# A two-layer decoder block on one core: the last sublayer's p product taken out of the expert loop and parked in DRAM, gates by f32r, one-hots turned by spread ranks

## The chip, the cores and the metric

The kernel runs on one core of one Trainium2 chip. The time is that of one execution on the device in microseconds (us); the time of the kernel before is the median of three runs. The profile is of one further execution, taken by the hardware profiler. In it PE is the matrix engine, PEld its weight loads, DVE the vector engine, ACT the scalar engine, POOL the general-purpose engine, and SP the engine that here does nothing but issue DMAs. A "q" behind a name (SPq) is that engine's sequencer.

## What is computed

Two transformer blocks of width 1024 over 512 tokens. The change lies in the second half of the second block: a mixture of experts (32 experts of hidden size 512 in 4 groups; each token goes to 2 experts of one group) and behind it a sublayer that adds a gated product of a second input `p` (256 features per token).

```python
x = x + merged @ w_out[i]                         # end of the mixer
h = rmsnorm_2(x, g_ffn[i])
x = x + hier_moe(h, w_grp[i], w_exp[i], w1[i], w3[i], w2[i])
h = rmsnorm_2(x, g_ple[i])
x = x + jax.nn.sigmoid(h @ w_pg[i]) * (p[i] @ w_ple[i])   # last sublayer
return rmsnorm_2(x, g_final)
```

`hier_moe` is, for each token, gate-weighted `(silu(x @ w1[e]) * (x @ w3[e])) @ w2[e]` over its two experts. The product `p @ w_ple` depends on inputs alone, so it may be computed at any time before the last sublayer.

## The kernel before

Activations lie feature-major: 8 tiles of 128 features x 512 tokens (`KT` is 8). Outside the experts a product is made of three matmuls of 4-byte operands in the reduced format f32r (`mm3`: high x high, low x high, high x low), after each operand has been split into a high and a low part: the high part by a cast on ACT, the low by a subtraction (`split`, `split_to`), on DVE unless told otherwise. `fm` makes one 128 x 512 output tile this way; with 8 input tiles it takes 24 matmuls, with 2 it takes 6. The raw weights come by SP into a ring of three tiles (`raw`), their halves lie in rings `wh` and `wl` of three.

Four stages bear on the change, in order of time:

- **End of the mixer.** For each of 8 output tiles `m`, `fm` multiplies by `w_out2`; `done(m)` adds the result to `X`, forms the normed tile `hf`, multiplies it by the router's weights (`logits`), turns it (`htr`, four transposes) and splits the turned tile into `ht` (ACT high, DVE low). Here a scheduler sets the order on every engine.
- **Router.** `ltr` turns the logits to token-major; a chain of some 35 small DVE operations picks group and experts (`first_max`), ends in the 0/1 matrix `Mb`, and after the `rank` matmuls gives `rk`, the place of each token in its expert's list, or a number over 900 where it is not in it. `GM` holds each token's gate for each expert and its norm.
- **Expert loop.** From here to the end of the loop PE's order is the order written in the code (`_InOrder`). Experts go in 16 pairs. `gather` compares `rk` with 0..63 for four experts, which gives the one-hots `dh` (tokens x slots), and multiplies `ht` by them (64 matmuls for a group of two pairs): the tokens of each expert in 64 slots, `xg`. Pair `p` then runs `hidden(p)` (`h`: with `w1` and `w3` as moving operand in full f32, two matmul instructions for each; two experts side by side in the columns of the array), `outputs(p-1)` (`y`, with `w2`), `hidden_turned(p)` (`hidt`), half of the next group's `gather`, half of the `combine` of the last two pairs (`comb`, which scatters the results back with `dt`, the turned one-hots, and adds them to `X`), `turned(p)` (`dtr`: four transposes of the one-hots and a DVE copy to `dt`), and `gates_of(p+1)` (`gate`: four f32 matmuls of the one-hots with the 33 columns of `GM`). In pairs 14 and 15, where no gather is left, its place is taken by `ple_proj`, the product `p @ w_ple` (`fm` of 24 matmuls in each), whose raw operands SP has loaded into the `raw` ring during the loop and DVE and ACT have split into three expert tiles.
- **Last sublayer.** `last` multiplies by `w_pg`, takes the sigmoid, multiplies by `ple[m]`, norms, and writes out.

The experts' weights are 192 blocks of 1 MB (12 for a pair), in the order of use. `expert_tile` deals out 11 tiles of 1 MB in turn (8 `slot`, 3 `aux`), so a block is loaded when the block 11 before it has been used. Blocks 0 to 16 are loaded ahead: 0, 1 and 4 to 12 into the 11 tiles, block 2 into an `x8` tile, 3 and 13 to 16 in halves into ring tiles that are free by then. All these loads stand in SP's one queue, in which an issue that waits for its tile holds up all behind it.

Of the kernel before, what the change touches and what calls it, by code (L numbers as in the profile page):

```python
# [20 lines left out]
P = 128  # L21
S = 512
# [24 lines left out]
CSTS = ["ident", "iota", "riota", "negones", "dist", "cdist", "rowok", "qscale"]  # L47
CSTN = [128, 64, 8, 128, 512, 4 * NCMP, 1, 4]
NKEPT = sum(CSTN[:3])
# [4 lines left out]
def _constants():  # L54
# [15 lines left out]
    put("iota", np.tile(np.arange(64), (P, 1)))  # L70
    put("riota", np.tile(8.0 - np.arange(8), (P, 1)))
# [105 lines left out]
def _build(ctx, tc, nc, A, out, probe, stop):  # L177
# [479 lines left out]
    def compress(i):  # L657
# [25 lines left out]
        gt = work.tile([P, 62], F32, tag="gelt", bufs=1, name="gelt")  # L683
# [603 lines left out]

    def done(m, pt):
# [13 lines left out]
        V.tensor_tensor(ht[1][:, :, fs], p3, ht[0][:, :, fs].bitcast(F32), ALU.subtract)  # L1302
# [11 lines left out]
    for m in range(KT):  # L1314
        done(m, fm(loadw(A["w_out2"][m]), y))
# [8 lines left out]

    rT = rt("rT")
# [5 lines left out]
    lfm = tmp("lfm")  # L1331
    SC.copy(lfm[:36], pl[:36])
    pt = s_ps("ltr")
    for t in range(4):
        T.transpose(pt[:, t * 36:t * 36 + 36], lfm[:36, t * P:t * P + P], ident[:36, :36])
    L = tmp("L")[:, :144].rearrange("p (t e) -> p t e", t=4)
    V.tensor_copy(L, pt[:, :144].rearrange("p (t e) -> p t e", t=4))

# [14 lines left out]
    gsel = rt("gsel", 4, 8)  # L1353
    V.tensor_tensor(gsel, L[:, :, 4:36].rearrange("p t (g e) -> p t g e", g=4),
                    goh.unsqueeze(3).to_broadcast([P, 4, 4, 8]), ALU.mult)
    sel = rt("sel", 8)
# [4 lines left out]
    oh12 = rt("oh12", 8)  # L1361
# [8 lines left out]
    pr = s_ps("rank")  # L1370
# [8 lines left out]


    pg = rt("pg")
    gd = rt("gd", 4)
# [15 lines left out]
    GM = rt("GM", NE + 1)  # L1398
    outer(GM[:, :, 0:NE], oh1)
    V.tensor_copy(GM[:, :, NE], rT)  # L1400
# [10 lines left out]
    slot_tags = itertools.cycle(4 * ["slot"] + na * ["aux"] + (ns - 4) * ["slot"])  # L1411

    def expert_tile(kt=4, c=512, dt=F32):
        return slot("mw", dt, next(slot_tags)).rearrange("p a b -> p (a b)").rearrange("p (k c) -> p k c", k=kt)
# [10 lines left out]
    def expert_load(ap):  # L1425
        w = expert_tile(*ap.shape[1:])
        nc.sync.dma_start(w, ap)
        return [w[:, k] for k in range(ap.shape[1])]
# [6 lines left out]

    def ring_tile(tag):
        return ring.tile([P, 1024], F32, tag=tag, bufs=3, name="mw")
# [9 lines left out]
    for n in (0, 1, 4, 5):  # L1447
        ahead[n] = expert_load(aps[n])
    ahead[3] += half_load(ring_tile("raw"), aps[3][:, 2:4])
    for n in range(6, 13):  # L1450
        ahead[n] = expert_load(aps[n])
# [314 lines left out]
```

## Time and profile before

| | us |
|---|---|
| median of three runs (1817.0 to 1819.53) | 1817.97 |
| profiled execution, own time | 1818.39 |
| its span (first to last instruction) | 1816.6 |
| PE busy | 1747.1 |
| PE loading weights (beside PE) | 1255.6 |
| DVE busy | 839.6 |
| ACT busy | 625.6 |
| POOL busy | 127.6 |

PE is busy 96% of the span, so the few stretches in which it waits, and the work that it does, are what time can come from. A matmul's own duration in the trace includes its way through the array, during which the next one already runs; the pace of a row of matmuls is read from the distance of their starts. The expert loop lies between about 1257 and 1746 us; DMA moves 12 to 13 MB for each pair of experts in it.

### The profile page before, as it was taken

What the parts mean: (1) busy time and instruction counts of PE and PEld (TensorE: products, weight loads), DVE (VectorE), ACT (ScalarE), POOL (GpSimd) and SP (SyncE); (2) the same over time, 40 slices, a digit from 0 to 9 for tenths busy, and PEclk for the clock granted to TensorE, in tenths of its full rate; (3) what the DMA queues carried; (4) which work ended last, traced back from release to release, by engine and by line L of the source; (5) the groups of instructions that cost most, each with busy time, mean ns of one, the idle gap of its engine ahead of it and who ended that gap; (6) DMA issues with size and microseconds to landing.
All of it is one profiled execution on the core that took longest, in us unless ns stands there. A gap on an engine that the chain in (4) does not pass through costs nothing. (4 is left out here: it accounts for less than half of the span.)

```text
span 1816.6 us, 22448 instructions
## 1 busy us (share of the span) xinstructions
PE 1747.1 (96%) x8936; PEld 1255.6 (69%) x8937; DVE 839.6 (46%) x1551; ACT 625.6 (34%) x1100; POOL 127.6 (7%) x152
## 2 busy tenths in 40 slices
PE   6999999899999999999999999997999999999896
PEld 4887777678888888888877887865454545454466
DVE  5676787895553333333653522743122222221256
ACT  4356777653332222222553434321110101011143
POOL 1100000551000000001100100200000000000030
PEclk9999999999999999999999999998999999999998
DMA  7532221773232333333531332345899999999831
GB/s 301 155 112 70 58 59 70 255 266 116 70 116 93 98 100 93 96 90 94 173 94 50 103 95 93 128 139 214 344 417 414 418 417 419 416 420 393 325 116 52
DMA packets 69998, 342.90 MB, mean 189 GB/s; under 512 B 7936, under 2 KB 10528, under 8 KB 45824
## 3 DMA queue, kind: packets, MB, share of 16 engines
q1 hardware_dynamic: 66736, 334.87, 50.0%
q0 software_dynamic: 2432, 5.77, 1.5%
q8 instruction: 72, 1.18, 0.3%
q10 hardware_dynamic: 720, 0.77, 0.1%
q14 instruction: 38, 0.31, 0.1%
HBM read 333.51 MB, written 2.10 MB: 185 GB/s over the span
## 5 line engine op out<-in xcount | busy, mean ns | idle before, releaser
L261 DVE TENSOR_TENSOR wl<-raw,wh 128x1024 fp32r<-128x1024 f32 (+1 forms) x185 | 238.5, 1291 | 297.8 <-ACT wh L261 294.0
L273 PE MATMUL fm<-hh,wh 128*128 128x512 f32 (+1 forms) x944 | 362.7, 385 | 3.6 <-ACT hh L467 2.0
L274 PE MATMUL fm<-hl,wh 128*128 128x512 f32 (+1 forms) x944 | 361.6, 383 | 2.1 <-DVE hl L468 1.6
L275 PE MATMUL fm<-hh,wl 128*128 128x512 f32 (+1 forms) x944 | 361.7, 384 | 1.1 <-DVE wl L261 1.1
L261 ACT CAST wh<-raw 128x1024 fp32r<-128x1024 f32 (+1 forms) x187 | 193.5, 1037 | 476.3 <-PE fm L274 264.9
L155 PE MATMUL h<-mw,x 128*64 128x512 f32 x1016 | 223.3, 594 | 0.0
L273 PEld LDWEIGHTS fm<-hh,wh 128*128 128x128 f32 x944 | 179.0, 190 | 39.1 <-issue 3.2
L275 PEld LDWEIGHTS fm<-hh,wl 128*128 128x128 f32 x944 | 178.7, 190 | 36.1 <-DVE wl L261 2.2
L274 PEld LDWEIGHTS fm<-hl,wh 128*128 128x128 f32 x944 | 179.0, 190 | 35.6 <-DVE hl L468 2.5
L155 PEld LDWEIGHTS h<-mw,x 128*64 128x64 f32 x1016 | 71.9, 137 | 135.6 <-issue 135.0
L155 PE MATMUL y<-mw,hT 128*64 128x512 f32 x512 | 115.2, 599 | 4.8 <-DMA mw<-in_w 4.8
L1540 DVE SCALAR_TENSOR_TENSOR hs<-h,gt,hs 128x512 f32<-128x512 f32 x16 | 12.0, 750 | 203.3 <-PE h L155 203.3
L155 PEld LDWEIGHTS y<-mw,hT 128*64 128x64 f32 x512 | 37.0, 139 | 79.4 <-issue 73.7
L1570 ACT CAST ywh<-y 128x512 fp32r<-128x512 f32 x30 | 17.6, 586 | 189.2 <-PE y L155 189.2
L1490 DVE TENSOR_TENSOR X<-comb,X 128x512 f32<-128x512 f32 x64 | 44.0, 690 | 62.8 <-PE comb L155 62.8
L1041 PE MATMUL fm<-hidh,wl 128*128 128x512 f32 (+1 forms) x188 | 71.8, 382 | 0.0
L1039 PE MATMUL fm<-hidh,wh 128*128 128x512 f32 (+1 forms) x188 | 71.6, 381 | 0.0
L1040 PE MATMUL fm<-hidl,wh 128*128 128x512 f32 (+1 forms) x188 | 71.6, 381 | 0.0
L234 ACT ACTIVATE hs<-h,gt 128x512 f32<-128x512 f32 x16 | 11.0, 687 | 173.0 <-PE h L155 173.0
L274 PE MATMUL tm<-wl,hh 128*128 128x512 f32 (+2 forms) x192 | 65.1, 339 | 2.5 <-DVE wl L261 2.5
L155 PE MATMUL gath<-dh,hh 128*128 128x256 f32 x256 | 64.4, 293 | 2.2 <-DVE cnt L1403 2.2
L275 PE MATMUL tm<-wh,hl 128*128 128x512 f32 (+2 forms) x192 | 65.3, 340 | 0.0
(434 smaller groups left out, 2786.4 us busy)
## 6 DMA issues: line engine op xcount, KB each, us to landing
mw<-in_w SPq DMA_DIRECT2D x186, 1024.0 KB, 10.7
wa<-in_w_ada SPq DMA_DIRECT2D x24, 1024.0 KB, 6.8
raw<-in_w_merge SPq DMA_DIRECT2D x32, 512.0 KB, 3.6
raw<-in_w_in SPq DMA_DIRECT2D x28, 512.0 KB, 3.9
raw<-in_w_gate SPq DMA_DIRECT2D x22, 512.0 KB, 3.5
raw<-in_w_up SPq DMA_DIRECT2D x22, 512.0 KB, 3.5
raw<-in_w_v SPq DMA_DIRECT2D x16, 512.0 KB, 3.6
raw<-in_w_proj SPq DMA_DIRECT2D x16, 512.0 KB, 3.6
```

Of the source, the lines that this page charges most:

```text
L155: self._put(self.eng.matmul(*a, **k))
L234: i = SC.activation(*a, **k)
L261: last_split[:] = copy(h, src).ins, sub(l, src, h.bitcast(F32)).ins
L273: T.matmul(pt, ah, bh, start=first, stop=False)
L274: T.matmul(pt, ah, bl, start=False, stop=False)
L275: T.matmul(pt, al, bh, start=False, stop=last)
L1039: T.matmul(pt[:, cs], wh[:, k], hid[0][:, n, cs], start=(n == 0), stop=False, skip_group_check=True)
L1040: T.matmul(pt[:, cs], wh[:, k], hid[1][:, n, cs], start=False, stop=False, skip_group_check=True)
L1041: T.matmul(pt[:, cs], wl[:, k], hid[0][:, n, cs], start=False, stop=(n == FT - 1), skip_group_check=True)
L1490: V.tensor_tensor(X[:, m], po, X[:, m], ALU.add)
L1540: V.scalar_tensor_tensor(hs, pt, st["gt"][:, 0:1], hs, ALU.mult, ALU.mult)
L1570: SC.copy(yh[:, n], ys[n])
```

## The change

- `ple_proj` moves from pairs 14 and 15 of the loop to the end of the mixer. It is a generator now, and `step` puts pieces of three matmuls between the last product of the mixer and the first gather: 6 matmuls before the last tile's `logits`, 3 before `ltr`, 21 before `rank`, 18 before `gather`. Its operands are loaded behind `w_out2` and split into the ordinary rings, the low parts by POOL. ACT copies each of the 8 result tiles into one slot tile and two `raw` tiles, and POOL writes them to a DRAM tile `pled` by eight DMAs of 256 KB. At the last sublayer SP reads `pled` back by two DMAs of 1 MB.
- PE's written order begins before `w_out2`, with `fm(m)` ahead of `done(m-1)`. `ltr` stands ahead of `ssT`, and the low part of `ht` for the last tile is made behind the first one-hots `dh0`, which are compared in four pieces.
- `gates_of`: `GM` is split into high and low f32r halves side by side, 66 columns, and multiplied by the one-hots in f32r: four matmuls. ACT copies the high half, DVE adds the low.
- `turned`: instead of transposing one-hots, the ranks are turned once (`rkT`, 32 experts x 512 tokens, in pair 0). For a pair, POOL spreads two columns of the identity over 64 columns each (`of`); one f32r matmul with `rkT` puts each expert's ranks on 64 partitions, and DVE compares them with the partition's number (`icol`) to give `dt`.
- The tiles of the expert weights are dealt in another order (`aux` first), and after the first 11 a twelfth block, in two `raw` halves, joins the turn.

```diff
+    def ple_proj():
+        raws = [load(a) for a in (A["p"], A["w_ple"][0], A["w_ple"][1])]
+        pf, *ws = [split(r, sub=G.tensor_sub) for r in raws]
+        t_ = slot("ple")
+        outs = [t_[:, i] for i in range(4)]
+        for t_ in (ring_tile("raw"), ring_tile("raw")):
+            outs += [t_[:, i * S:i * S + S] for i in range(2)]
+        for m in range(KT):
+            pt = next(banks)("ple")
+            for k in range(2):
+                n = 2 * (m % 4) + k
+                mm3(pt, ws[m // 4][0][:, n], ws[m // 4][1][:, n], pf[0][:, k], pf[1][:, k], k == 0, k == 1)
+                yield
+            SC.copy(outs[m], pt)
+            G.dma_start(pled[:, m], outs[m])
...
-    for m in range(KT):
-        done(m, fm(loadw(A["w_out2"][m]), y))
+    T = _InOrder(tc, nc.tensor)
+    pts = [fm(loadw(A["w_out2"][0]), y)]
+    for m in range(1, KT):
+        pts.append(fm(loadw(A["w_out2"][m]), y))
+        done(m - 1, pts[m - 1])
+
+    pler = ple_proj()
+    step(pler, 2)
+    done(KT - 1, pts[KT - 1])
+    step(pler, 1)
...
+    step(pler, 7)
...
+    dh0 = onehot()
+    for t in range(4):
+        i = V.tensor_tensor(dh0[:, t], rk[:, t, 0:4].unsqueeze(2).to_broadcast([P, 4, SLOTS]),
+                            K("iota").unsqueeze(1).to_broadcast([P, 4, SLOTS]), ALU.is_equal)
+    tc.add_manual_dep(subs[-1].ins, i.ins.name, order)
+    for _ in pler:
+        pass
...
+    GM = rout.tile([P, 4, 2 * (NE + 1)], F32R, name="GM")
+    V.tensor_copy(GM[:, :, :NE + 1], gm_)
+    V.tensor_tensor(GM[:, :, NE + 1:], gm_, GM[:, :, :NE + 1].bitcast(F32), ALU.subtract)
...
-    slot_tags = itertools.cycle(4 * ["slot"] + na * ["aux"] + (ns - 4) * ["slot"])
+    slot_tags = itertools.chain(na * ["aux"] + ns * ["slot"],
+                                itertools.cycle(na * ["aux"] + ns * ["slot"] + ["raw"]))
...
     def gates_of(p):
...
-            T.matmul(pgt[:, 0:NE + 1], dq[:, t].rearrange("p e s -> p (e s)"), GM[:, t],
+            T.matmul(pgt[:, 0:2 * n], dq[:, t].rearrange("p e s -> p (e s)"), GM[:, t],
                      start=(t == 0), stop=(t == 3))
+        gs = mix.tile([P, n], F32, tag="gs", bufs=1, name="gs")
+        SC.copy(gs, pgt[:, 0:n])
+        V.tensor_tensor(gs, pgt[:, n:2 * n], gs, ALU.add)
...
     def turned(p):
...
         pt = s_ps("dtr")
-        for t in range(4):
-            T.transpose(pt[:, t * P:t * P + P], dq[:, t].rearrange("p e s -> p (e s)"), ident)
+        of = tmp_r("of")[:, :P]
+        G.tensor_copy(of.rearrange("p (e s) -> p e s", e=2),
+                      ident[:, 2 * p:2 * p + 2].unsqueeze(2).to_broadcast([P, 2, SLOTS]))
+        T.matmul(pt, of, rkT, start=True, stop=True)
         pairs[p]["dt"] = mix.tile([P, S], F32R, tag="x2", bufs=3, name="dt")
-        V.tensor_copy(pairs[p]["dt"], pt)
+        V.tensor_scalar(pairs[p]["dt"], pt, K("icol"), None, ALU.is_equal)
...
-            nxt = gather(p // 2 + 1, sts[p // 2 + 1]) if p < NP - 2 else ple_proj(raws) if p < NP else iter(())
-        if p == NP - 4:
-            raws = ple_loads()
+            nxt = gather(p // 2 + 1, sts[p // 2 + 1]) if p < NP - 2 else iter(())
...
+    for i, t_ in enumerate((x8(4, S), expert_tile(4, S))):
+        nc.sync.dma_start(t_, pled[:, 4 * i:4 * i + 4])
+        ple.extend(t_[:, n] for n in range(4))
```

Three places of the built program show the moves. First PE from the last tile's `logits` to the first `gather`; before:

```order
L1295 MATMUL logits<-hf,wr 36x512
L1298 MATMUL htr<-cst,hf 128x128 x4
L1328 MATMUL ssT<-ones,acc 128x1 x4
L1335 MATMUL ltr<-cst,lfm 128x36 x4
L1373 LDWEIGHTS triub
L1373 MATMUL rank<-Mb,triub 128x32
...
L155 MATMUL gath<-dh,hh 128x256
```

and in the changed program, where each `ple` row that is shown stands for the first of its run (6, 3, 21 and 18 rows):

```order
L156 MATMUL ple<-wh 128x512
...
L156 MATMUL logits<-hf,wr 36x512
L159 MATMUL htr<-cst,hf 128x128 x4
L156 MATMUL ple<-wh 128x512
...
L159 MATMUL ltr<-cst,lfm 128x36 x4
L156 MATMUL ssT<-ones,acc 128x1 x4
L156 MATMUL ple<-wh 128x512
...
L156 MATMUL rank<-Mb,triub 128x32
...
L156 MATMUL ple<-wh 128x512
...
L156 MATMUL gath<-dh,hh 128x256
```

PE has matmuls of the p product between the steps for which it waited on DVE's chain before.

Second, PE at the end of the loop, from `hidt` of pair 14 to `h` of pair 15; before:

```order
L158 MATMUL hidt<-cst,hs 128x128 x4
L155 MATMUL fm<-mw 128x512 x24
L155 MATMUL comb<-dt,ywh 128x512
...
L158 MATMUL dtr<-cst,dh 128x128 x4
L155 MATMUL gate<-GM,dh 128x33 x4
```

and in the changed program:

```order
L159 MATMUL hidt<-cst,hs 128x128 x4
L156 MATMUL comb<-dt,ywh 128x512
...
L156 MATMUL dtr<-rkT,of 128x512
L156 MATMUL gate<-GM,dh 128x66 x4
```

The 24 matmuls of the p product are gone (as in pair 15), and the four transposes have become one matmul.

Third, SP's queue around the start of the loop, with what an issue waits for (DMAHW and DMASW are landings of transfers of the hardware queues and of POOL's software queue); before, with block 9 as `mw_9972` and the two halves of block 16 last among the loads ahead:

```order
L253 DMA raw_9812<-in_w_out2 128x1024 [waits DMAHW3_49,DVE_49]
L1433 DMA mw_9964<-in_w1 128x1024 [waits DMAHW5_49,DMAHW1_49,DVE_49]
...
L1427 DMA mw_9972<-in_w1 128x2048 [waits PE_49]
...
L1427 DMA mw_9978<-in_w3 128x2048 [waits DMAHW3_49,PE_49]
L1433 DMA mw_9992<-in_w2 128x1024 [waits DMAHW4_49]
L1433 DMA mw_9994<-in_w2 128x1024 [waits DMAHW5_49]
L1677 TENSOR_LOAD cnti_9949 [waits DVE_49,PE_49,Activation_49]
L1427 DMA mw_10218<-in_w2 128x2048 [waits DMAHW6_49,PE_49]
```

and in the changed program, with block 12 as `mw_10077` and the halves of block 13 as `mw_10079` and `mw_10081`:

```order
L254 DMA raw_9850<-in_w_ple 128x1024 [waits DMAHW3_49,DVE_49]
L1496 DMA mw_10061<-in_w3 128x2048 [waits Pool_49]
...
L1502 DMA mw_10067<-in_w1 128x1024 [waits DMAHW6_49,Pool_49]
L1496 DMA mw_10069<-in_w1 128x2048 [waits DMAHW4_49,PE_49]
...
L1496 DMA mw_10077<-in_w3 128x2048 [waits DMASW2_49,DMASW3_49,DMASW1_49,DMAHW0_49,DMASW0_49,Activation_49]
L1502 DMA mw_10079<-in_w3 128x1024 [waits DMASW5_49,DMAHW1_49,DMASW4_49,Activation_49]
L1502 DMA mw_10081<-in_w3 128x1024 [waits DMASW7_49,DMAHW2_49,DMASW6_49,Activation_49]
L1502 DMA mw_10083<-in_w3 128x1024 [waits DMAHW3_49,PE_49]
...
L1496 DMA mw_10328<-in_w2 128x2048 [waits DMAHW1_49,PE_49]
```

The loads of `p` and `w_ple` stand ahead of blocks 5 to 12, and blocks 12 to 16 stand behind the landing of the eight writes to `pled`. In the loop itself `p` and `w_ple` are no longer in the queue.

## Rows read from the trace of the kernel before

**Rows 1.** The page, part 1: busy time of each engine, share of the span, instructions.

```profile
PE 1747.1 (96%) x8936; PEld 1255.6 (69%) x8937; DVE 839.6 (46%) x1551; ACT 625.6 (34%) x1100; POOL 127.6 (7%) x152
```

**Rows 2.** Stretches: length; busy us by engine (PE, PEld, DVE, ACT, POOL); granted clock, DMA, GB/s.

```profile
1240.00:1250.00 10.00, 4.55 (x33) 4.48 (x34) 5.72 (x30) 1.70 (x3) 0.00 (x0) 0.50 0.48 195
1261.00:1311.00 50.00, 49.07 (x274) 23.43 (x272) 8.76 (x16) 4.89 (x8) 0.00 (x0) 1.00 0.85 329
1334.00:1666.00 332.00, 332.00 (x1763) 167.25 (x1762) 77.06 (x138) 33.34 (x55) 0.00 (x0) 1.00 1.01 417
1350.00:1360.00 10.00, 10.00 (x64) 6.30 (x61) 1.98 (x3) 2.33 (x4) 0.00 (x0) 1.00 1.02 425
```

**Rows 3.** PE's waits from 1180 us on: total, times, longest.

```profile
PE rank L1373 <- DVE Mb L1365: 5.6, 1, 5.6
PE y L155 <- DMA mw<-in_w: 4.8, 1, 4.8
PE gath L155 <- DVE cnt L1403: 2.2, 1, 2.2
PE logits L1295 <- DVE hf L1294: 1.3, 1, 1.3
```

**Rows 4.** PE in order of time, first gather: start, duration, instruction, count [idle before].

```profile
1246.00 0.55 PE L155 MATMUL gath<-dh,hh 128*128 128x256 f32 x1 [2.15 <-DVE cnt L1403]
...
1252.11 0.33 PE L155 MATMUL gath<-dh,hh 128*128 128x256 f32 x1
...
1256.36 0.97 PE L155 MATMUL gate<-GM,dh 128*128 128x33 f32 x8
```

**Rows 5.** PE in order of time, one pair in the middle of the loop.

```profile
1515.29 13.95 PE L155 MATMUL h<-mw,x 128*64 128x512 f32 x64
...
1536.45 0.36 PE L155 MATMUL gath<-dh,hh 128*128 128x256 f32 x1
...
1540.27 0.39 PE L155 MATMUL comb<-dt,ywh 128*128 128x512 f32 x1
...
1544.12 0.60 PE L158 MATMUL dtr<-cst,dh 128*128 128x128 f32 x4
1544.56 0.98 PE L155 MATMUL gate<-GM,dh 128*128 128x33 f32 x8
1545.47 13.95 PE L155 MATMUL h<-mw,x 128*64 128x512 f32 x64
```

**Rows 6.** PE in order of time, pairs 14 and 15.

```profile
1679.95 7.04 PE L155 MATMUL y<-mw,hT 128*64 128x512 f32 x32
...
1687.33 5.74 PE L155 MATMUL fm<-mw 128*128 128x512 f32 x24
1692.91 0.40 PE L155 MATMUL comb<-dt,ywh 128*128 128x512 f32 x1
...
1716.83 8.56 PE L155 MATMUL y<-mw,hT 128*64 128x512 f32 x32 [4.77 <-DMA mw<-in_w]
...
1725.73 5.84 PE L155 MATMUL fm<-mw 128*128 128x512 f32 x24
1731.41 0.39 PE L155 MATMUL comb<-dt,ywh 128*128 128x512 f32 x1
...
1742.27 3.65 PE L155 MATMUL y<-mw,hT 128*64 128x512 f32 x14
```

**Rows 7.** DMA issues: SP at the loop's start; POOL's queue and the loop's loads (KB, landing).

```profile
1260.95 1.08 SPq L1427 DMA_DIRECT2D mw<-in_w  x2
...
qd<-qd POOLq DMA_DIRECT2D x8, 256.0 KB, 3.7
...
mw<-in_w SPq DMA_DIRECT2D x132, 1024.0 KB, 11.6
```

**Rows 8.** POOL's splits of `w_pg` (mean ns); DVE's low part between `L` and the chain.

```profile
L261 POOL TENSOR_TENSOR wl<-raw,wh 128x1024 fp32r<-128x1024 f32 x2 | 4.7, 2360 | 556.1 <-PE dtr L158 556.1
...
1237.91 0.68 DVE L1302 TENSOR_TENSOR hl<-htr,hh 128x512 fp32r<-128x512 f32 x1
```

More of the change, by code (lines that the diff above doesn't have):

```diff
@@ L682, in compress @@
         T.transpose(pt[:, :62], gel, ident[:62, :62])
-        gt = work.tile([P, 62], F32, tag="gelt", bufs=1, name="gelt")
+        gt = tmp("gelt")[:, :62]
         V.tensor_copy(gt, pt[:, :62])
@@ L1286, in _build, with ring_tile @@
     pl = o_ps("logits")
+    subs = []
+    dram = ctx.enter_context(tc.tile_pool(name="dram", bufs=1, space=bass.MemoryType.DRAM))
+    pled = dram.tile([P, KT, S], F32, name="pled")
+    def ring_tile(tag):
+        return ring.tile([P, 1024], F32, tag=tag, bufs=3, name="mw")
+    def ple_proj():
[13 more added lines that the diff above has]
+            G.dma_start(pled[:, m], outs[m])
     def done(m, pt):
@@ L1323, in rt, with rv @@
         return rout.tile([P, 4, *shape], F32, name=name)
+    lfm = tmp("lfm")
+    SC.copy(lfm[:36], pl[:36])
+    pt = s_ps("ltr")
+    for t in range(4):
+        T.transpose(pt[:, t * 36:t * 36 + 36], lfm[:36, t * P:t * P + P], ident[:36, :36])
+    rtmp = tmp("rtmp")
+    used = [0]
+    def rv(*shape):
+        n = 4 * int(np.prod(shape))
+        v = rtmp[:, used[0]:used[0] + n]
+        used[0] += n
+        if len(shape) == 1:
+            return v.rearrange("p (t a) -> p t a", t=4)
+        return v.rearrange("p (t a b) -> p t a b", t=4, a=shape[0])
+    L = rv(36)
+    V.tensor_copy(L, pt[:, :144].rearrange("p (t e) -> p t e", t=4))
     rT = rt("rT")
@@ L1369, in _build @@
     outer(Mb, oh12)
-    pr = s_ps("rank")
+    pr = o_ps("rank")
     for t in range(4):
@@ L1425, in expert_load @@
     def expert_load(ap):
-        w = expert_tile(*ap.shape[1:])
+        tag, kt = next_tag(True), ap.shape[1]
+        if tag == "raw":
+            return [w for i in range(2) for w in half_load(ring_tile(tag), ap[:, i * kt // 2:(i + 1) * kt // 2])]
+        w = slot("mw", F32, tag).rearrange("p a b -> p (a b)").rearrange("p (k c) -> p k c", k=kt)
         nc.sync.dma_start(w, ap)
-        return [w[:, k] for k in range(ap.shape[1])]
+        return [w[:, k] for k in range(kt)]
     def half_load(tile_, ap):
@@ L1446, in _build @@
     ahead[3] = half_load(mix.tile([P, 1024], F32, tag="x4", bufs=2, name="mw"), aps[3][:, 0:2])
[L1447 to L1450, printed above, removed]
+    for n in (0, 1, *range(4, 13)):
+        if n == 8:
+            ahead[3] += half_load(ring_tile("raw"), aps[3][:, 2:4])
         ahead[n] = expert_load(aps[n])
@@ L1573, in _build @@
     ple = []
-    def ple_loads():
-        return [load(a) for a in (A["p"], A["w_ple"][0], A["w_ple"][1])]
-    def ple_proj(raws):
-        def split_slot(r):
-            _, kt, c = r.shape
-            t_ = expert_tile(2, 1024, F32R)
-            w = [t_[:, i, :kt * c].rearrange("p (k c) -> p k c", k=kt) for i in range(2)]
-            split_to(*w, r)
-            return w
-        pf, *ws = [split_slot(r) for r in raws]
-        for t_ in (x8(4, S), expert_tile(4, S)):
-            ple.extend(t_[:, i] for i in range(4))
-        for m in range(KT):
-            SC.copy(ple[m], fm(ws[m // 4], pf, 2 * (m % 4), 2))
-            yield
-    T = _InOrder(tc, nc.tensor)
     sts = [{} for _ in range(NG + 1)]
@@ L1673, in _build @@
     last(hb, acc, x6, ws)
-    dram = ctx.enter_context(tc.tile_pool(name="dram", bufs=1, space=bass.MemoryType.DRAM))
     most = nc.values_load(cnti[0:1, NE:NE + 1], min_val=0, max_val=S)
```

77 lines of the change are left out of this document (43 added, 34 removed).

## The prediction

> **What bounds the kernel now.** I read the page first, for who is busy: PE is, for 96% of the span [rows 1], so time can come only from work that PE no longer does, from matmuls that become shorter, or from the few stretches in which it waits. Then the list of PE's waits, for how much of that there is in the part that the change touches: 5.6 us for `Mb` ahead of `rank`, 4.8 for a weight in a `y`, 2.2 ahead of the first gather, 1.3 ahead of `logits` [rows 3]; 13.9 us in all. Then PE in order of time, for the length of one pair and of each piece in it: from one `h` to the next 1515.29 to 1545.47, 30.18 us, without an idle column [rows 5]. Last the stretches, for the engine that PE would wait for if it were faster, the weights' DMA: over 1334 to 1666 its share is 1.01, and 417 GB/s flow [rows 2]. In those 332 us 132 loads of 1 MB were issued [rows 7], one in 2.515 us, and a pair needs twelve: 30.18 us. So in the loop PE and the stream are level. Every microsecond that PE saves per pair must come out of the lead that the loads have.
>
> The profiled execution took 1818.39 us, its span is 1816.6; 1.8 us lie outside. The median of the runs is 0.4 below it. The sum below stands against 1818.4 and I leave the 0.4 out.
>
> **The change part by part.**
>
> (a) The p product leaves the loop. `fm` to `comb` is 1687.33 to 1692.91, 5.58 us, and 1725.73 to 1731.41, 5.68 us [rows 6]: **−11.3**. 5.58 us for 24 matmuls is also the pace of one f32r matmul of 512 columns, 0.2325 us.
>
> (b) The wait of 4.77 us in the `y` of pair 14 [rows 6]. That weight came late because three loads for the product stood in SP's queue and its split parts took three tiles of the turn; both are gone. The `y` itself took 8.56 there and 7.04 one pair before, so 1.5 more was lost inside it: **−6.3**. What could be late next is the stream as a whole; see (f).
>
> (c) `turned` and `gates_of`, in each of 16 pairs. `dtr` to `gate` is 1544.12 to 1544.56, 0.44 us; one matmul of 512 columns instead is 0.23: −0.2. `gate` to `h` is 0.91 for four f32 matmuls [rows 5]. The nearest row for an f32r matmul with few columns and weights of its own is the gather: 32 matmuls of 256 columns from 1536.45 to 1540.27, 0.119 each [rows 5]. Four with 66 columns: 0.48 at most by that row, −0.44. The bounds: nothing saved, if f32r at 66 columns goes no faster than f32 at 33; or, a quarter of the columns of the gather's row, hardly anything left. I take the gather's row, since the loading of 128 columns of weights is the same in both. 16 x 0.64: **−10.2**, between −3 and −17. Once, four transposes turn the ranks: +0.4. Hidden beside this: POOL's spreading of the identity has PE's whole combine ahead of it (3.85 us, 1540.27 to 1544.12), and its tile comes free with the `y` before; the largest POOL row here, 2.36 us for 128 x 1024 [rows 8], bounds it for 128 x 128. If that cover went, 16 x 2.4 would be lost. ACT's copy of 33 columns and DVE's addition have the 14 us of `h` before the gates are wanted. DVE compares where it copied.
>
> Against `dtr` as a matmul speaks a rule of the Trainium skill, "Perfetto Trace Analysis", section on transposes under the optimization of tensor performance: logical transposes should use transpose, not a standard matmul, because arithmetic is then skipped. Here four transposes of 128 columns take 0.44 us and a matmul of 512 columns 0.2325 [rows 5, 6], so the trace speaks against the rule; by it the term would lose its 3.2 us, and the sum would end 3.2 higher.
>
> (d) The head. 48 matmuls of the product now stand between `logits` and the first gather: 48 x 0.2325 = 11.2 us. They stand exactly where PE waits: 1.3 + 5.6 + 2.2 = 9.1 us [rows 3]. DVE's chain, which sets these waits, gets shorter by the low part of `ht` (0.68 us) [rows 8], which moves behind the first one-hots. One more gain: after those waits the granted clock is 0.50 in 1240 to 1250 (the 1.2 GHz level) [rows 2], and the first 28 matmuls of the gather took 1246.00 to 1252.11, 0.218 each, against 0.119 in the loop [rows 4, 5]. With PE busy ahead of them they would take 3.3 us instead of 6.1: −2.7. In sum 11.2 − 9.1 − 0.7 − 2.7 + 0.4 for pieces that don't fit their gap exactly = −0.9; I take **−1**, with −3 to +8: the upper end is the product with only a third of it hidden. ACT's splits of `p` and `w_ple` and POOL's (2.36 us for each 1024 columns [rows 8], three of them) are due when the product begins, and their loads stand behind the last `w_out2`, some 20 us earlier.
>
> (e) Parking `ple`. Eight writes of 256 KB by POOL's queue; such a DMA landed 3.7 us after its issue [rows 7]. Blocks 12 to 16 of the weights now wait for them and go out from about 1254 instead of before 1246. Block 12 is wanted only when pair 1 begins, one pair after the loop's start (1257.27), about 1285. SP's queue behind them holds the releases of the loop, the first at 1260.95 [rows 7]. No cost on PE; the price in the stream is in (f). At the end 2 MB are read back, 5 us of stream after the last weight; `ple` is wanted only after the first 24 matmuls of `w_pg`: +0.5.
>
> (f) The stream. Loads of the loop begin at 1260.95, and in 1261 to 1311 the DMA share is 0.85 [rows 2]: 7.5 us idle. 175 blocks x 2.515 = 440 us. So the last block could have landed at 1261 + 7.5 + 440 = 1708.6 at the same rate; blocks 12 to 16, no longer all landed by 1246, add up to 5. The last half of the last `y` takes 3.5 after that: its end is at 1712 to 1717 by the stream. By PE, the old end is 1742.27 + 3.65 = 1745.9 [rows 6], less 11.3, 6.3, 9.8 and 1: 1717.5. The two ends meet, so the stream gives a little back where a release comes late: **+1.5** (0 to 6). A twelfth tile (two `raw` halves) and the new turn let it run further ahead, which is why I take a low value.
>
> For that rate, the Trainium skill ("DMA: Bandwidth & Descriptors", the section Measured) has 341 GB/s for a transfer of 1 MB and 425 for 16 MB. By 341 a pair would take 37 us, which the 30.18 of the loop exclude; by 425 it would take 29.6, and the sum would be some 1.5 lower; the best 10 us of the loop show 425 too [rows 2].
>
> The sum: −11.3 − 6.3 − 10.2 + 0.4 − 1 + 0.5 + 1.5 = −26.4, from 1818.4: **1792.0 us**. What is left of the program behind the loop, 70.7 us, is as before.
>
> **The rivals.**
>
> *The stream binds fully.* For it: share 1.01 over 332 us [rows 2], and PE's pair becomes 29.5 against 30.18 of twelve loads. Against it: the idle 7.5 us at the start and a lead of eleven blocks, 27 us, against which PE gains only 16 x 0.64. Then nothing of (c) is cashed after the lead is used, say two thirds of it lost: 1792 + 6.5 = 1798.5.
>
> *The head isn't hidden.* The product's pieces wait for POOL's splits or stand in DVE's way, and the 9.1 us of waiting stay beside 11.2 us of work: 1792 + 9 = 1801. For it: the order on PE is fixed, so one late split holds up `logits`, and with it the chain. Against it: the raw loads have some 20 us of lead.
>
> *The gates and the transposes don't do what they say.* f32r at 66 columns costs what f32 at 33 does, and one f32r matmul what four transposes do: (c) is lost, and with it the stream's give-back: 1792 + 10.2 − 1.5 = 1800.7. For it there is no row with so few columns; against it the gather's pace.
>
> *Slower.* SP's queue is held: block 12 and, behind it, each release of the loop wait for the eight writes. If these complete one after another, the last lands at about 1242 + 8 x d. From d = 3 us (1266, past the first release, 1260.95) each microsecond more delays the stream by one. With the margin between the stream's end and PE's nearly nil, it costs nearly one for one: for a loss of 28 us the last must land at about 1294, d = 6.5: 1820. For it: software queue, 256 KB to DRAM. Against it: 3.7 us from issue to landing for the same size and queue [rows 7], with issues six matmuls (1.4 us) apart.
>
> **How the numbers follow.** The forecast has 0.60, the stream 0.15, the head 0.11, the gates 0.09, slower 0.05. The forecast's own bounds: head −3 gives 1790, gates at their best −17 can't be cashed because of the stream; (f) at nothing 1790.5; both together 1788.5, and a little for the clock: low 1787. Up: the stream, the head and the gates lie at 1798.5 to 1801: high 1801.5. That leaves out slower and the tails of the rest. A measurement of this kernel tells about 0.2%, 3.6 us, from no change; all cases but the last are well past it: faster 0.93, the same 0.03 (part of the last case, and the head and the stream together), slower 0.04.
>
> **What would show it.** In the profile of the changed kernel: no p product between `hidt` and `comb` of pairs 14 and 15; the waits of PE ahead of `rank`, `gath` and `logits` under 1 us each and the granted clock 1.00 in the ten microseconds ahead of the first gather, with gather matmuls of 0.12; the first `h` at about 1256; `dtr` one matmul of 0.23, `gate` to `h` under 0.5; a pair of 29.5 us at first, later drawn to 30.2; last `y` ending near 1719. Waits of `h` or `y` on DMA of more than 3 us in sum would mean the stream rival; PE waiting on POOL or ACT at a piece of the product, the head; `gate` still at 0.9, the third; SP waiting for POOL's writes past 1266, the last. The forecast is wrong if the tail behind the loop grows, which I hold at 70.7 us without a row for the new order there.

## The result, and the profile after

| | before | changed kernel |
|---|---|---|
| median of six runs each, same chip (us) | 1818.58 (1815.91 to 1822.74) | 1793.22 (1790.41 to 1797.95) |
| ratio, with its 95% interval | | 0.986 (0.9843 to 0.9878) |
| profiled execution, own time | 1818.39 | 1793.39 |
| its span | 1816.6 | 1791.7 |

The changed kernel is faster by 25 us (1.4%); forecast were 1792.0, between 1787.0 and 1801.5. The page of the changed kernel, part 1, answers to [rows 1]:

```profile
PE 1738.7 (97%) x8828; PEld 1246.8 (70%) x8829; DVE 844.2 (47%) x1570; ACT 629.2 (35%) x1116; POOL 145.8 (8%) x180
```

PE lost 8.4 us of busy time but 25 us of span: two thirds of the gain, 16.5 us, is time in which it had been idle. PE's waits from 1150 us on (total, times, longest; those ahead of `ss` and `fm` lie in the last sublayer) answer to [rows 3]:

```profile
PE ss L453 <- DVE acc L446: 4.3, 1, 4.3
PE fm L275 <- DVE mw L465: 1.6, 2, 1.2
PE y L156 <- DMA mw<-in_w: 0.8, 1, 0.8
PE rank L156 <- DVE Mb L1410: 0.4, 1, 0.4
```

The waits ahead of `logits` and of the first gather are gone, that ahead of `rank` fell from 5.6 to 0.4, and the `y` of pair 14 still waits for a weight, 0.8 where it was 4.8. Stretches (length; busy us and instructions of PE, PEld, DVE, ACT, POOL; granted clock, DMA share, GB/s), the second, fourth and fifth to be held against [rows 2] (there the middle of the loop goes to 1666), the others from either side of the parking:

```profile
1229.00:1239.00 10.00, 10.00 (x48) 6.33 (x47) 6.04 (x8) 3.95 (x6) 3.26 (x3) 1.00 0.16 35
1240.00:1250.00 10.00, 9.64 (x59) 7.96 (x58) 8.08 (x46) 5.72 (x10) 3.27 (x6) 1.00 1.00 409
1249.00:1259.00 10.00, 10.00 (x80) 8.78 (x80) 0.56 (x4) 3.03 (x6) 1.35 (x3) 1.00 1.00 389
1261.00:1311.00 50.00, 49.61 (x270) 22.92 (x268) 9.46 (x19) 5.96 (x11) 0.59 (x2) 1.00 1.00 404
1334.00:1660.00 326.00, 326.00 (x1689) 161.10 (x1687) 77.66 (x151) 35.45 (x66) 3.27 (x11) 1.00 1.01 420
```

In the router the granted clock is 1.00 (the 2.4 GHz level) where it was 0.50. From 1240 us to the end of the loop the DMA is full, but for a dip to 0.84 between 1258 and 1262; the 15% that it was idle in 1261 to 1311 before are used, in part by the halves of blocks 13 to 16, which land there until 1273 and had landed ahead of the loop before. PE in order of time (start, duration, instruction, count), the last piece of the product and the first gather, to be held against [rows 4]:

```profile
1248.86 0.39 PE L156 MATMUL ple<-wh,wl 128*128 128x512 f32 x1
1249.09 0.28 PE L156 MATMUL gath<-dh,hh 128*128 128x256 f32 x1
...
1252.40 0.28 PE L156 MATMUL gath<-dh,hh 128*128 128x256 f32 x1
...
1256.66 0.53 PE L156 MATMUL gate<-GM,dh 128*128 128x66 f32 x4
1257.12 3.65 PE L156 MATMUL h<-mw,x 128*64 128x512 f32 x16
```

The first 28 gather matmuls take 3.31 us, where they took 6.11. And a pair in the middle, against [rows 5]:

```profile
1509.66 13.95 PE L156 MATMUL h<-mw,x 128*64 128x512 f32 x64
...
1538.54 0.39 PE L156 MATMUL dtr<-rkT,of 128*128 128x512 f32 x1
1538.77 0.53 PE L156 MATMUL gate<-GM,dh 128*128 128x66 f32 x4
1539.23 10.95 PE L156 MATMUL h<-mw,x 128*64 128x512 f32 x50
```

`dtr` to `gate` is 0.23, `gate` to `h` 0.46, and the pair 29.57 instead of 30.18. The end of the loop, against [rows 6]:

```profile
1697.61 4.17 PE L156 MATMUL y<-mw,hT 128*64 128x512 f32 x17
1702.58 3.65 PE L156 MATMUL y<-mw,hT 128*64 128x512 f32 x14 [0.80 <-DMA mw<-in_w]
1706.16 0.66 PE L159 MATMUL hidt<-cst,hs 128*128 128x128 f32 x4
...
1716.65 3.65 PE L156 MATMUL y<-mw,hT 128*64 128x512 f32 x14
```

The last `y` ends at 1720.3 (1719 was forecast). By stages, with marks that both programs have (the first matmul with `w_out2`, the first `h`, the `h` of pairs 14 and 15):

| stage | before | after | difference |
|---|---|---|---|
| up to the first matmul with `w_out2` | 1177.5 | 1178.4 | +0.8 |
| head: from there to the first `h` | 79.74 | 78.76 | −1.0 |
| pairs 0 to 13 | 408.89 | 400.38 | −8.5 |
| pair 14, to the `h` of 15 | 31.94 | 26.05 | −5.9 |
| from there to the end | 118.48 | 108.16 | −10.3 |
| outside the span | 1.8 | 1.7 | −0.1 |

### The profile page after: what moved, and what is told of

The parts are those of the page before. It is cut to its first block, busy times and chain, and to the rows that moved or that the text cites. A ratio compares the mean times of both kernels' runs of the same rounds, so it can differ in the third digit from the quotient of the medians.

```text
span 1791.7 us, 22379 instructions
## 1 busy us (share of the span) xinstructions
PE 1738.7 (97%) x8828; PEld 1246.8 (70%) x8829; DVE 844.2 (47%) x1570; ACT 629.2 (35%) x1116; POOL 145.8 (8%) x180
## 5 line engine op out<-in xcount | busy, mean ns | idle before, releaser
L274 PE MATMUL tm<-wh,hh 128*128 128x512 f32 (+2 forms) x192 | 65.1, 339 | 0.0
L1650 DVE TENSOR_TENSOR ywl<-y,ywh 128x512 fp32r<-128x512 f32 x30 | 20.6, 686 | 89.6 <-ACT ywh L1649 89.6
```

What stands on the lines that cost most here:

```text
L274: T.matmul(pt, ah, bh, start=first, stop=False)
L1650: V.tensor_tensor(yl[:, n], ys[n], yh[:, n].bitcast(F32), ALU.subtract)
```

## The experiments

Each was timed beside the kernel before. An interval of some 0.0015 to 0.0025 in the ratio is 3 to 4.5 us, and between profiled executions the part of the program ahead of the change ended at anything from 1176.2 to 1182.5 us. So sizes of one or two us are read from the traces, between marks. "Loop" is from the first `h` to the start of the last `y`, "y14" the length of the `y` of pair 14 without a wait ahead of it (6.97 where nothing waits in it), "pair" is one pair in the middle of the loop, "landed" the last weight's landing after the first `h`; all in us.

| kernel | ratio | head | pair | y14 | loop | landed |
|---|---|---|---|---|---|---|
| before | 1 | 79.74 | 30.17 | 8.49 | 478.52 | 475.86 |
| changed | 0.986 | 78.76 | 29.57 | 8.83 | 453.98 | 455.40 |
| old_gates | 0.9877 | 79.21 | 30.00 | 6.97 | 458.65 | 455.31 |
| old_turn | 0.9874 | 78.75 | 29.77 | 6.97 | 455.36 | 455.84 |
| ple_move_only | 0.9901 | 79.20 | 30.22 | 6.97 | 462.07 | 457.25 |
| c_only | 0.9949 | 79.30 | 29.57 | 9.68 | 470.36 | 466.64 |
| no_product | 0.984 | 76.62 | 29.57 | 6.97 | 452.13 | 453.21 |
| product_first | 0.9889 | 86.97 | 29.57 | 6.97 | 452.10 | 453.06 |
| comb_high | 0.9839 | 78.76 | 28.17 to 29.89 | 10.93 | 452.57 | 454.91 |
| fewer_bytes | 0.9821 | 78.78 | 29.57 | 6.97 | 452.11 | 443.27 |
| writes_x3 | 0.994 | 78.76 | 29.89 | 10.92 | 468.34 | 469.77 |
| eleven_tiles | 0.9869 | 78.76 | 29.57 | 8.26 | 453.41 | 454.82 |
| lead_tail | 0.9854 | 78.78 | 29.57 | 8.05 | 453.18 | 454.58 |

### The small products

**old_gates**

```diff
-            T.matmul(pgt[:, 0:2 * n], dq[:, t].rearrange("p e s -> p (e s)"), GM[:, t],
+            T.matmul(pgt[:, 0:NE + 1], dq[:, t].rearrange("p e s -> p (e s)"), GM[:, t],
```

with `dq` and `GM` in f32 and the gates taken from `pgt`, as before the change.

> The changed kernel with one part undone: the gates by four f32 matmuls with 33 columns again. My theory (PE sets the end of the loop, the weight stream is just level with it): gate to h grows from 0.46 to 0.91 us in every pair, 16 x 0.45 = +7.2, of which the 0.8 us that a y waits for a weight in the changed kernel is given back: +6.4, about 1799.6 on the scale of before = 1818.4. Rival, the stream of weights already sets the loop's end in the changed kernel: no more than +1, and the wait of y for a weight gone.

Ratio 0.9877 (0.9863 to 0.9892). **old_turn**

```diff
-        T.matmul(pt, of, rkT, start=True, stop=True)
+        for t in range(4):
+            T.transpose(pt[:, t * P:t * P + P], dq[:, t].rearrange("p e s -> p (e s)"), ident)
```

> The changed kernel with one part undone: the one-hots turned by four transposes and a copy again, no turned ranks. My theory: dtr to gate grows from 0.23 to 0.44 us, 16 x 0.21 = +3.4, less 0.4 for the ranks that are not turned and less the 0.8 us wait for a weight: +2.2, about 1795.4. Rival, the rule that transposes are the cheaper form: no change or a gain (1793 or less). Rival, the stream sets the end: +0 to +0.5.

Ratio 0.9874 (0.986 to 0.9888). PE in order of time in a middle pair, first of old_gates, then of old_turn:

```profile
1540.74 0.39 PE L156 MATMUL dtr<-rkT,of 128*128 128x512 f32 x1
1540.97 0.97 PE L156 MATMUL gate<-GM,dh 128*128 128x33 f32 x8
1541.88 8.37 PE L156 MATMUL h<-mw,x 128*64 128x512 f32 x38
```

```profile
1539.35 0.60 PE L159 MATMUL dtr<-cst,dh 128*128 128x128 f32 x4
1539.70 0.61 PE L156 MATMUL gate<-GM,dh 128*128 128x66 f32 x4
1540.25 10.09 PE L156 MATMUL h<-mw,x 128*64 128x512 f32 x46
```

The f32 gates cost 0.91 again and a pair 0.43 more; the transposes cost 0.35 for 0.23, the gates behind them 0.55 for 0.46, and a pair 0.20 more. In both kernels the wait in y14 is gone, so of 6.9 us (16 x 0.43) old_gates loses 5.1 in head and loop together (6.4 were expected), and old_turn of its 3.1 (up to the `h` of pair 15) only 1.4. By time, old_gates is 3 us slower than the changed kernel and old_turn 2.5, each known to about 3 us only: the sizes are the traces'. **ple_move_only** makes both edits.

> The changed kernel with both small products undone (f32 gates and transposed one-hots), so that the move of the p product, the parking and the new turn of the tiles stand alone. My theory: the parts add up, +7.2 + 3.4 - 0.4 - 0.8 = +9.4: about 1802.6, and no wait of y for a weight. Rival, the stream sets the end of the changed kernel: 1794 to 1796.

Ratio 0.9901 (0.9886 to 0.9915), 7.5 us above the changed kernel by ratio, 8.5 by head and loop. The parts add up once it is seen that each edit alone gives back the same loss in y14: 6.9 + 3.3 − 1.9 = 8.3. The stream does not set the loop of the changed kernel as a whole, or these kernels would have cost nothing.

**gate_34**

```diff
-            T.matmul(pgt[:, 0:2 * n], dq[:, t].rearrange("p e s -> p (e s)"), GM[:, t],
+            T.matmul(pgt[:, 0:n + 1], dq[:, t].rearrange("p e s -> p (e s)"), GM[:, t, :n + 1],
...
-        V.tensor_tensor(gs, pgt[:, n:2 * n], gs, ALU.add)
```

> The changed kernel with only the high parts of the gates, 34 columns instead of 66 (the low parts of the gates are left out). If the loading of the one-hots as weights sets the price of a gate matmul, as in the gather, gate to h stays at 0.46 us; if the columns set it, it falls to 0.25.

PE in order of time in a middle pair:

```profile
1541.32 0.39 PE L156 MATMUL dtr<-rkT,of 128*128 128x512 f32 x1
1541.55 0.51 PE L156 MATMUL gate<-GM,dh 128*128 128x34 f32 x4
1541.99 1.51 PE L156 MATMUL h<-mw,x 128*64 128x512 f32 x6
```

0.44 us with 34 columns, 0.46 with 66: the columns hardly count. The low parts of the gates cost PE next to nothing, and the row of the gather (0.119 for a matmul with 128 x 128 weights of its own) was the right one to size the term by.

**c_only** is the kernel before with the new gates and the turned ranks (and with the router's temporaries packed as in the changed kernel):

```diff
 (before)
+    def gates_of(p):   # as in the changed kernel
+    def turned(p):     # as in the changed kernel
```

> The kernel before with only the f32r gates and the ranks turned once (the p product stays in pairs 14 and 15, the old turn of eleven tiles). Theory A, the 4.8 us wait of the y in pair 14 comes from what stands in SP's queue (the loads of p and w_ple and their splits): it stays near 4.8 and the saving of 9.7 us is cashed in full, about 1808.5. Theory B, that wait is where a stream that cannot go faster catches up with PE: what PE saves comes back as a longer wait there, 4.8 + up to 8, about 1813 to 1817.

Ratio 0.9949 (0.9935 to 0.9964): −9.3 us, 1808.5 to 1809 where theory A said 1808.5. PE's two longest waits from 1170 us on, and then the stretch of y14 in the kernel before:

```profile
PE rank L1386 <- DVE Mb L1378: 5.7, 1, 5.7
PE y L156 <- DMA mw<-in_w: 4.9, 1, 4.9
```

```profile
1700.00:1710.00 10.00, 10.00 (x50) 3.31 (x48) 0.00 (x0) 1.97 (x2) 0.00 (x0) 1.00 0.38 138
1710.00:1720.00 10.00, 5.23 (x18) 1.43 (x16) 0.75 (x1) 0.00 (x0) 0.00 (x0) 0.83 0.68 263
```

The weight wait stays 4.9. The whole y14 grows by 1.2, and that is the clock, not the stream: behind the wait the granted clock is at its 1.2 GHz level (0.50 from 1706 to 1710 in c_only), two matmuls that start side by side then take 0.85 us instead of 0.43, and c_only has six such pairs at the start of its y14 where the kernel before has three. The rows above show what the wait is: in the ten us ahead of it the DMA share is 0.38. The block that y14 waits for was issued at 1712.08, when the `h` of pair 15 had ended and set its tile free, 10.3 us behind the block ahead of it in SP's queue, and landed 4.7 us later; in c_only, too, it is issued at the end of that `h`. So the wait belonged to the order of queue and tiles with the p product in them, not to a stream at its limit, and step (b) had the right cause.

### The head

**no_product**

```diff
-                mm3(pt, ws[m // 4][0][:, n], ws[m // 4][1][:, n], pf[0][:, k], pf[1][:, k], k == 0, k == 1)
                 yield
-            SC.copy(outs[m], pt)
+            SC.copy(outs[m], pf[0][:, 0].bitcast(F32))
```

> The changed kernel without the 48 matmuls of the p product (loads, splits, copies, the writes to DRAM and the reading back stay; what is parked is p's high part, so the last sublayer's product is left out). My theory, the product is hidden in the head: PE's waits ahead of logits, rank and the first gather come back, 8 to 9 us in sum, the granted clock falls to about a half at the first gather (which costs 2 to 3 us), and the first h starts within 1.5 us of where it does now: 1792 to 1794.5. Rival, the product is not hidden: 11.2 us less, 1782.

Ratio 0.984 (0.9815 to 0.9866), or 1789 on the scale of before = 1818.4, under the range expected; the head is 2.1 us shorter, not 11.2 and not 0 to 1.5. PE's waits in the head, ten microseconds of it, and the first and the 29th gather matmul:

```profile
PE rank L156 <- DVE Mb L1408: 5.0, 1, 5.0
...
PE gath L156 <- DVE dh L1429: 1.3, 1, 1.3
```

```profile
1234.00:1244.00 10.00, 3.56 (x34) 2.72 (x33) 7.85 (x44) 3.41 (x8) 0.29 (x1) 0.75 0.99 406
```

```profile
1243.46 0.55 PE L156 MATMUL gath<-dh,hh 128*128 128x256 f32 x1 [1.28 <-DVE dh L1429]
...
1249.46 0.28 PE L156 MATMUL gath<-dh,hh 128*128 128x256 f32 x1
```

Without the product PE waits 6.3 us, 5.9 more than with it, the granted clock of the stretch falls to 0.75, and the first 28 gather matmuls take 5.99 us instead of 3.31. 5.9 + 2.7 = 8.6 of the product's 11.2 us are paid by this; that leaves 2.6, and 2.1 are found. The product is hidden for four fifths. What is new: this head, with its cold gather and no product, is still 3.1 us shorter than that of the kernel before. The wait of 1.3 ahead of `logits` does not come back (it went with PE's written order, `fm(m)` ahead of `done(m-1)`), the chain is 0.9 shorter between `rank` and the gather, and the f32r gates give 0.45. The end is also 1.9 us nearer because y14 waits no more: without the product the writes go out earlier, and the last has landed 13 us ahead of the first `h`, where it landed 1.2 us behind it.

**product_first**

```diff
-    step(pler, 2)
+    for _ in pler:
+        pass
     done(KT - 1, pts[KT - 1])
```

> The changed kernel with all 48 matmuls of the p product ahead of the last tile's logits, so that none lies beside the vector engine's chain. My theory: the waits ahead of rank and gather return (5.2 + 3 us less what the chain still hides) with the lower clock at the gather (2.7 us): the first h 9 to 11 us later, and the end 8 to 11 us later, 1801 to 1804. Rival, the cover is not what counts (only the place in the loop was the cost): 1793 to 1795.

Ratio 0.9889 (0.9865 to 0.9913), some 5 us above the changed kernel; the head is 8.2 us longer (86.97), with the same waits as no_product (5.0 and 1.3), a granted clock of 0.73 and 5.44 us for 28 gather matmuls. The loop gives 1.9 back, since the weights have the longer time to land. So the price of losing the cover is 8.2 in the head, less than the 9 to 11 expected: 5.9 us of waiting came back, not 8.2, and the gather matmuls cost 2.1 more, not 2.7. The time, some 1798 on the scale of before = 1818.4, is under the 1801 to 1804 expected.

### The stream of weights

**comb_high**

```diff
-            parts = [(y_, pairs[p]["dt"]) for p in ps_ for y_ in pairs[p]["y"]]
+            parts = [(y_, pairs[p]["dt"]) for p in ps_ for y_ in pairs[p]["y"][:1]]
```

> The changed kernel without the low parts in the combine (half of its matmuls are left out: 1.9 us of PE for each pair, 31 us in all with the last ones). My theory, the stream of weights is level with PE: next to nothing of the loop's 30 us is cashed, the loop ends when the last weights have landed, PE waits for weights from the middle of the loop on; gain 1 to 4 us: 1789 to 1792. Rival, the stream has a lead: -25 to -30, 1763 to 1768.

Ratio 0.9839 (0.9815 to 0.9863), by the interval not to be told from the changed kernel's, where PE had some 27 us less to do in the loop (half of the combine's 3.85 us in 14 pairs). PE's waits from 1170 us on, and the middle of the loop:

```profile
PE y L156 <- DMA mw<-in_w: 7.4, 9, 1.4
PE comb L156 <- DVE X L1558: 5.9, 14, 1.1
...
PE h L156 <- DMA mw<-in_w: 1.9, 2, 1.3
```

```profile
1334.00:1660.00 326.00, 318.47 (x1621) 153.59 (x1619) 75.42 (x151) 35.45 (x66) 3.23 (x11) 1.00 1.01 420
```

The DMA was at 1.01 and 420 GB/s as it was before the edit, PE is idle 7.5 us in this stretch, and its pair goes from 28.17 early in the loop to 29.89 late: twelve loads of 1 MB at 2.49 us. The loop is shorter by 1.4 us only, and behind the start of the last `y` 2.4 us are lost (82.97 to the end, for 80.61), which was not looked into: by the profiled executions nothing is gained, and the 1 to 4 us expected are not shown. A faster PE gains nothing here.

**fewer_bytes**

```diff
+        loads[0] += 1
+        if loads[0] % 4 == 0:
+            nc.sync.dma_start(w[:, :kt // 2], ap[:, :kt // 2])
+            return [w[:, k % (kt // 2)] for k in range(kt)]
```

> The changed kernel in which of every fourth weight block only one half is loaded and used twice (a part of the weights is left out, the number of matmuls is unchanged): about an eighth less to load. My theory: PE sets the end once the stream is relieved, so only the 0.8 us wait of a y goes, 1792 to 1793.5, and the DMA share in the loop falls below 0.95. Rival, the stream sets the end: faster by more than 4 us.

Ratio 0.9821 (0.9798 to 0.9845), 7 us below the changed kernel; 5.6 by the two profiled executions. The stretches of the loop:

```profile
1261.00:1311.00 50.00, 49.61 (x270) 22.91 (x268) 9.46 (x19) 5.95 (x11) 0.59 (x2) 1.00 0.87 342
1334.00:1660.00 326.00, 326.00 (x1691) 161.13 (x1689) 77.53 (x151) 35.41 (x66) 3.23 (x11) 1.00 0.94 378
```

By the number the rival's sign (more than 4 us) came. By the stages it is not the loop: the share fell as expected and y14 is 6.97, 1.9 us shorter; that is all that the loop gives, and the pair stays at 29.57. My expectation missed the other 3.6 us, which come behind the start of the last `y` (76.98 to the end instead of 80.61). There PE has another order in this kernel (the last `y` as a whole, where the changed kernel has four matmuls of the combine inside it), and the last weights have landed 12 us earlier, and with them the loads of `w_pg` behind them.

**lead_tail** was to collect both.

```diff
-    T = nc.tensor
     banks = wide
...
     for _ in combine((NP - 2, NP - 1), fin):
         pass
+    T = nc.tensor
...
+        held.append(ring_tile("raw"))
         t_ = slot("ple")
...
-            ahead[3] += half_load(ring_tile("raw"), aps[3][:, 2:4])
+            ahead[3] += half_load(held[0], aps[3][:, 2:4])
```

> The changed kernel with two further edits. The half block that holds up SP's queue for the third split of POOL gets the raw tile that p's split frees first, so that the blocks behind it go out about 4 us earlier; and PE keeps the written order through the last combine (y of pair 15 as a whole, then the combine). If the stream of weights sets what PE waits for in the y of pair 14 (a loss of 1.9 us in that y, of which 0.8 stands in the list of waits), that loss goes. If the interleaved order behind it costs what the run with fewer bytes suggests, the end of the program comes 3.4 us sooner after the last h begins. Both: about 1788 on the scale of before = 1818.4, ratio 0.983. Rival, neither is on the path: 1793.

Ratio 0.9854 (0.9835 to 0.9873), not to be told from the changed kernel's. SP's waits from 1195 us on show that the first half of the edit did nothing: the queue stood behind POOL's split as long as in the changed kernel, whose row reads the same 19.0.

```profile
SPq L1503 <- POOL wl L262: 19.0, 1, 19.0
...
SPq L1497 <- DMA pled<-ple: 13.2, 2, 10.7
```

The order in the tail is worth 1.1 us (79.55 behind the start of the last `y`). What makes the other 2.6 us of fewer_bytes was not separated: that they come from the earlier loads of the last sublayer is an argument, not a measurement.

**writes_x3**

```diff
-            G.dma_start(pled[:, m], outs[m])
+            for d_ in (pled, *more):
+                G.dma_start(d_[:, m], outs[m])
```

> The changed kernel in which each of the 8 tiles of the parked product is written three times, to three places in DRAM (24 writes of 256 KB instead of 8): it prices the hold of SP's queue behind these writes and their share of the stream. My theory, the stream has no lead to absorb it: blocks 12 to 16 and all behind them go 8 to 12 us later, the loss in the y of pair 14 grows from 1.9 us to about 10: 1801 to 1804. Rival, the lead of the loads absorbs it: 1793 to 1794.

Ratio 0.994 (0.9922 to 0.9959): 14.5 us slower than the changed kernel. SP's queue in order of time (start, time to the last issue of the row, count), first of the changed kernel, then of this one; the fifth issue of the third row is block 12:

```profile
1213.64 0.33 SPq L254 DMA_DIRECT2D raw<-in_w_ple  x1
1214.02 1.75 SPq L1496 DMA_DIRECT2D mw<-in_w  x3
1215.82 20.77 SPq L1502 DMA_DIRECT2D mw<-in_w  x2
1236.69 16.14 SPq L1496 DMA_DIRECT2D mw<-in_w  x5
1256.23 3.77 SPq L1502 DMA_DIRECT2D mw<-in_w  x4
```

```profile
1219.74 20.86 SPq L1504 DMA_DIRECT2D mw<-in_w  x2
1240.70 23.59 SPq L1498 DMA_DIRECT2D mw<-in_w  x5
1271.51 10.13 SPq L1504 DMA_DIRECT2D mw<-in_w  x8
```

Blocks 13 to 16 begin at 1271.51, 10.4 us after this kernel's first `h` (1261.13), where they began 0.9 us ahead of it in the changed kernel (1256.23 against 1257.12): 11.3 us later, and the added writes take part of the DMA as well. The last weight lands 14.4 us later, and the loop is 14.4 longer: one for one, and nothing is absorbed. How much of this is the held queue the run does not tell: the 16 added writes carry 4.2 MB, 10 us of a stream at 420 GB/s (an estimate from these two figures), while the DMA share from 1272 to 1280, where the queue stood, is 0.54, which leaves 3.7 us idle.

**eleven_tiles**

```diff
-                                itertools.cycle(na * ["aux"] + ns * ["slot"] + ["raw"]))
+                                itertools.cycle(na * ["aux"] + ns * ["slot"]))
```

> The changed kernel without the twelfth block in the turn of the tiles (after the first round the raw tiles are not used). Theory A, the twelfth tile lets the stream run further ahead at the start of the loop: the DMA share of the first 50 us falls below 0.97 and the loss in the y of pair 14 grows by about one load, 2.5 us: 1795 to 1798. Theory B, the stream is full with eleven too: 1793 to 1794 and the share stays at 1.00.

Ratio 0.9869 (0.985 to 0.9888). The start of the loop and its middle:

```profile
1261.00:1311.00 50.00, 49.61 (x270) 23.14 (x271) 10.03 (x23) 5.94 (x12) 0.59 (x2) 1.00 0.96 387
1334.00:1660.00 326.00, 326.00 (x1687) 161.56 (x1687) 78.67 (x149) 35.41 (x66) 3.23 (x11) 1.00 1.01 421
```

y14 is 0.6 shorter rather than 2.5 longer, and the time is the same within the interval: theory B in what counts. The share at the start is 0.96, as theory A had it; this kernel's first `h` is 4.2 us later, though, and with the stretch moved by as much the share is 0.97 for 1.00. The twelfth tile buys nothing that can be measured in the time.

## Why the prediction was right

(a) **The product's 11.3 us.** The pieces are gone from pairs 14 and 15. Pair 14 gave 5.9 (5.58 of it the product; with (c) 6.2 were forecast), the stretch behind it 10.3, as the terms (a), (b), (c), (e) and (f) of that stretch add up to: −5.7 − 6.3 − 0.2 + 2.0 = −10.2. Measured there are −4.9 up to y14, +0.3 in it, −5.5 from there to the last `y`, and −0.2 behind its start.

(b) **The weight's wait.** Its cause is as the forecast had it: c_only and the idle DMA ahead of the wait show that it is not the stream's rate, and ple_move_only, where the product has moved and a pair takes 30.22 as before, has it no more. The 1.5 lost inside the `y` were the lower clock behind the wait (0.53 from 1716.8 to 1720). That another, smaller wait comes up in its place was put into (f).

(c) **Gates and turned ranks.** 0.61 us for each of the first 14 pairs, against 0.64 forecast with the once-made `rkT` beside it; old_gates and old_turn give 0.43 and 0.20. The choice between the ends (the gather's row, not the columns) was right, and gate_34 shows why. On the turn the Trainium skill ("Perfetto Trace Analysis", section on transposes) says to keep logical transposes as transposes; here a pair is 0.20 us longer with four of them than with one f32r matmul of 512 columns. The two do not do the same, though: the kernel has no need to turn a one-hot where it can make the turned one from a turned rank.

(d) **The head.** −1.0 was forecast and −1.0 came, which is in part luck: 0.45 of it belongs to term (c), since the first gate lies in the head (ple_move_only, with the old gates, has 79.20 there, −0.5). Two parts were also put down to the wrong thing. I counted all of the 9.1 us of waits as filled by the product. no_product shows that the 1.3 ahead of `logits` went with the written order, and that the gaps which the product fills are 5.9 us, with 2.7 from the clock as forecast. The product costs 2.1 us there, and the other edits of the head gain 3.1.

(e) **Parking.** The writes landed later than worked out: block 12 was issued at 1252.5, where 1254 was forecast, but the last write landed at 1258.3, eight us after its issue, beside a full DMA (389 GB/s); 3.7 us had been the price in [rows 7]. That the four blocks under way make the difference is not shown: in no_product six of the eight writes landed after 4.0 to 4.4 us with the DMA share at 1.00 too, the other two after 7.4 and 8.8. The next blocks went out from 1256.2. This is what makes the mechanism of the slower rival real, and writes_x3 shows that a later stream is paid one for one, though not how much of it the held queue does and how much the added bytes. It did not strike because the writes let go of the queue at 1258.5, before the tile of the loop's first load comes free (about 1260.8, if as in the kernel before it is 3.7 us behind the first `h`). The half blocks still in the queue put that load off to 1263.7, 6.6 us behind the first `h`; the DMA share of 0.84 from 1258 to 1262 shows what the stream lost in that stretch, some 0.6 us. The +0.5 for reading back can't be told apart: behind the end of the last `y` 71.4 us are left, where 70.7 and 0.5 were forecast, but the stretch from its start, with a part of the combine in it, is 0.9 shorter.

(f) **The stream's give-back.** 1.5 forecast; y14 lost 1.9 (8.83 against 6.97), of which the list of waits shows only 0.8. Where the pair takes 29.55 to 29.57 us, p is out of the loop and all bytes are loaded (changed, no_product, product_first, eleven_tiles, lead_tail, and gate_34, which is not in the table and ran once), this loss goes with the last weight's landing after the first `h`: 0 at 453.1 and 453.2, 0.7 at 454.0, 1.1 at 454.6, 1.3 at 454.8, 1.9 at 455.4. The trace shows the step: the last block that y14 needs landed 445.4 us after the first `h` in the changed kernel, and the `y` came to it at 443.7; in eleven_tiles it landed at 444.9, in no_product, which loses nothing, at 443.2. The pairs before were not drawn out to 30.2 as I had written: all take 29.57, a little less than twelve loads of 2.49 (29.9), and the lead covers the difference until pair 14.

By comb_high and writes_x3 the balance between PE and stream, worked out from 132 loads in 332 us, is real on both sides: the loop can hardly be shortened at PE any more (1.4 us for 27) and is lengthened at once by a later stream. The rate was 420 GB/s, not 417. The Trainium skill ("DMA: Bandwidth & Descriptors", the section Measured) has 341 GB/s for a transfer of 1 MB issued from GpSimd; the loads here are of that size, issued from SP, and run at 420 with several under way at once, so that figure does not bound them.

The twelfth tile, for which I took a low give-back, is no reason (eleven_tiles). That the DMA is full from the loop's start I put down to the loads' place in the queue, blocks 13 to 16 above all, and to p's loads being gone from the loop; this is an argument, and the two were not tried apart.

The rivals: the stream binds in one place, for 1.9 us, not fully; the head was hidden for four fifths; the gates did what they say; SP's queue was held by the writes until 1258.5, not past the first release.

## What to carry to other kernels

Before a product is moved into a gap, price the gap by leaving the product out: here 11.2 us of matmuls cost 2.1, because two waits and the lower clock behind them were paid anyway. When an engine and its stream of loads are nearly level, count the loads first: here a pair of 29.57 us stands against twelve loads of 29.9, and from there 27 us less of matmuls made the loop 1.4 shorter, while 16 more writes of 256 KB ahead of it made it 14.4 longer. Size a small matmul by a neighbour with the same weights to load, not by its columns.

## What was not expected

A wait for a weight in a `y` costs more than its row: 0.8 us stand in the list of waits, the `y` took 1.9 longer. By the starts of its matmuls the 19th comes 1.4 us late, since the row leaves out what the profile still counts as the matmul before. The rest is lost at the end: the matmuls of a `y` start in twos, one for each expert, 0.01 us apart and a pair each 0.43; behind the late block the twos are out of step, and the last two start 0.43 apart. A gate matmul took the same time with 34 and with 66 columns (0.44 and 0.46 us for four). And with next to no change ahead of it, the head begins anywhere from 1176.2 to 1182.5 us in these executions, a spread larger than most of the terms of the sum.
